# Unused filler tiles that shift where split weights and experts' operands begin in SBUF, modulo 128 bytes

## The chip, the core and the metric

The kernel runs on one NeuronCore of a Trainium2 chip. Its time is device time in microseconds (us): the median of the runs is 1857.83 us, over 3 runs from 1856.85 to 1857.92 us.

## The reference

Two transformer-like blocks follow each other on x of 256 tokens by 1024 features, all in float32. Block 1 has two layers of a token mix (a gated linear recurrence beside a latent attention) and a mixture of 16 experts, of which each token takes two of one group of four. Block 2 has a recurrent mixer, an MLP of width 4096, a local attention and a second MLP. Cut to what matters here, it is a long series of products with weights that are each used once:

```
h = rmsnorm(x, norm1_g[l]) * (1 + sc1) + sh1
x = x + g1 * token_mix(h, ..., w_in[l], ..., w_br_a[l], w_br_b[l], w_out[l])
...
he = silu(t @ w_gate[e]) * (t @ w_up[e])                 # for each expert
y  = y + combine[:, e:e+1] * (he @ w_down[e])
...
z = hn @ lru_w_in ;  x = x + g * ((scan * gelu(gate)) @ lru_w_out)
x = x + g * (square(relu(hn @ mlp_w1)) @ mlp_w2)         # twice
q, k, v, o of chunk_attention: hn @ w                     # once
```

## The kernel before, in words

**Weights.** A weight comes from HBM in pieces of 1 MiB, [128, 2048] in float32, into a tile `raw` of the pool `ring` (five buffers, and two more called `more` in the expert stages). `parts_of` (line 423) cuts a piece into parts of 1024 columns and splits each: ScalarE copies it to `whi` in float32r (line 436), VectorE subtracts that from the source and writes the rest to `wlo` (line 437). The parts take the three buffers of the pool `wsp` in turn; the recurrent stage has two more, in the pool `wse` (function `extra`), so that there three parts of five lie in `wsp`.

**Products.** Every operand is such a pair of a high and a low half, and a product is three matmuls: high by high, high by low, low by high (`mm3`, lines 447 to 449; `way_out`, lines 1654 to 1656; `first_linear`, lines 829 to 831). Each matmul has a weight load of its own ahead of it, 128 by 128, that TensorE's load queue (PEld) runs beside the matmul before it. One operand stands (it is loaded), the other moves (it is streamed):

- In `linear_gen` (names `ps_mm`), the bands (`ps_bd`), `way_out` (`acc`) and `first_linear` (`ps_f`) the weight `whi` or `wlo` stands and 256 columns of an activation move.
- In `linear_tok_gen` (`ps_mt`) the activation stands and the weight moves, 256 columns of it (512 in the two places of the latent attention, tile `cn_`).
- In the experts (`ps_e`, `py`) the gathered tokens `xg` or the turned hidden values `hT` stand and 512 columns of the weight move.

In the names of the profile the operand that moves stands first: `ps_mm<-h_hi,whi` has `whi` standing, `ps_e<-whi,xg` has `xg` standing.

**Order.** The program is written out once, in one order for each engine; the stages run one after the other, with the modulation units (`ada_unit`, line 325 on TensorE; `ada_dve`, line 299 on VectorE) put into numbered places by the table `FILL`.

**Where tiles lie.** Pools stack up in SBUF in the order in which they are opened, and within a pool each tile begins at the next multiple of 32 bytes of its partition. Nothing else sets where a tile begins. Adding up the sizes gives these beginnings modulo 128:

| tile | role | begins at, modulo 128 |
|---|---|---|
| `whi`, `wlo` of `wsp` | stand in linears, move in the experts and in `linear_tok_gen` | 64 |
| `whi`, `wlo` of `wse` (recurrent stage) | stand | 0 |
| `h_hi`, `h_lo`; `a_hi`, `a_lo` (MLP); `mg`; `hq`; `xc`; `cn_`; `y_hi` | move (`h` and `cn_` stand in `linear_tok_gen`) | 64 |
| `oa`, `ob`, `oo`, `y_lo` | move | 96 |
| `yo` | moves | 0 |
| `xg` of the first two expert groups | stands | 32 |
| `xg` of the last two, and `hT` | stand | 0 |

All slices that the products take begin whole multiples of 512 bytes further on, so that these numbers hold for them too. The small tiles `gh` (line 1123, 32 bytes, in the pool `mw`) and `q2s` (line 1754, 4 bytes) put the tiles that come after them 32 bytes off: that is how `oa`, `ob`, `oo` and `xg` come to 96 and 32.

Of the kernel before, what the change touches and what calls it, by code (L numbers as in the profile page):

```python
# [25 lines left out]
# ---------------------------------------------------------------- host layout  # L26
def cuts(kt, n):
    """The pieces a weight of kt row tiles and n columns streams in: (first row tile, row tiles, first column, columns)."""
    if kt <= 8:
        c = RING // kt // P * P  # L30
        return [(0, kt, c0, min(c, n - c0)) for c0 in range(0, n, c)]
    if kt == 11:
        return [(0, 11, c0, P) for c0 in range(0, n, P)]
    return [(k0, 8, c0, 2 * P) for c0 in range(0, n, 2 * P) for k0 in range(0, kt, 8)]


def pack(w):
    """Pieces of w, each as [128, row tiles, columns] in one row."""
    k, n = w.shape
# [5 lines left out]
# modulation units at the places in the program that have room for other than the usual number  # L45
# [11 lines left out]
def pack_mod(w, v0):  # L57
    """Four pieces for each 1024 columns of a modulation, each with two row tiles, or with two column tiles turned."""
# [45 lines left out]
def prepare(i):  # L104
# [30 lines left out]
    for l in range(DEPTH):  # L135
# [4 lines left out]
        # four heads at a time: the 32 that turn of each, then the 64 that stay  # L140
# [41 lines left out]
# ---------------------------------------------------------------- the program  # L182
def program(tc, A, out, dbg=None):
    nc = tc.nc
    from contextlib import ExitStack, nullcontext
    with ExitStack() as st:
# [3 lines left out]
        ring = pool("ring", 5)  # L190
        wsp = pool("wsp", 3)
        tmp = pool("tmp", 2)
# [5 lines left out]
        def banks(st_, stage, **tags):  # L198
            """The PSUM banks of a stage: a pool for each tag."""
# [12 lines left out]
        # ---- constants  # L212
# [45 lines left out]
        # ---- c  # L258
# [7 lines left out]
        def c_columns(i):  # L266
            """silu of a condition, 32 times"""
# [7 lines left out]
        def c_along(i):  # L275
            """silu of a condition along the free axis, on every partition"""
# [7 lines left out]
        # ---- ada: four units give the 1024 columns of a modulation, 256 in each column group of the array  # L284
# [3 lines left out]
        def ada_dve(u):  # L288
            """two column tiles of a modulation as sums along the free axis"""
# [43 lines left out]
        def ada_flush():  # L333
            """the turn of a modulation to columns, put off until the next unit's products have been queued"""
# [24 lines left out]
        def ada_site(n=1):  # L359
            """a place where units may come: the schedule says how many, n otherwise"""  # L360
# [13 lines left out]
        # ---- streaming of weights  # L374
        PRE, OWN, READY, GATE, LOADS, MORE = [], [], [], [], [], []

        def room():
            """the ring, with more buffers in turn where a stage has them"""
# [7 lines left out]
        def ready(pcs):  # L386
            """splits the next pieces that weights() will be asked for"""
# [3 lines left out]
        def prefetch(pcs):  # L391
            """loads the next pieces that weights() will be asked for"""
# [5 lines left out]
        def weights(ap, nk, nn):  # L398
            """A piece of nk row tiles and nn columns, split: w(k, c, n) -> (high, low)."""
# [16 lines left out]
        def extra(st_, n):  # L416
            """more room for split weights, in a stage that has it"""
# [42 lines left out]
        def linear_gen(pcs, kt, x, evac, fill=0, wide=False):  # L460
            """out^T tiles [128, 256]: weights stand, x (hi, lo) of [128, kt, 256] moves. With wide the first piece's
            tiles go together, for an x that is still being made."""
# [29 lines left out]
        def run(*gens):  # L492
            """Emits the generators to their ends, a step of each in turn."""
# [21 lines left out]
        def linear_tok_gen(pcs, kt, x, evac, wide=False):  # L515
            """token-major out [128 tokens, columns]: x stands, weights move."""
# [22 lines left out]
        # ---- norms  # L539
        def power(dst, src, mul=1.0):  # L540
            """(src * mul + eps) ** -1/2 of a small tile."""
# [3 lines left out]
        def rstd_tok(src, nk):  # L545
            """1/sqrt(mean + eps) of each token, [128 tokens, 2]; src(k) -> [128, 256]."""
# [11 lines left out]
        def spread(cols_):  # L558
            """columns of tokens (one for each token tile) -> [128, 256] along the free axis, in PSUM."""
# [11 lines left out]
        def stats_open(two=False, also=None, each=False):  # L571
            """The sums of squares of x, tile by tile as it gets its last sum; with two also those of x times final_g."""
# [26 lines left out]
        def stats_close(rt=None):  # L599
# [3 lines left out]
            if ST["two"]:  # L603
                ms = tmp.tile([P, 4], F32, tag="rm", name="rm")
                nc.vector.tensor_copy(ms, ST["ps"][:, 0:4])
                # r1 = (m1 + eps)^-1/2 and r1 (r1^2 m2 + eps)^-1/2 = (m2 + eps (m1 + eps))^-1/2
# [15 lines left out]
        def rstd_x(n=2):  # L622
            """the statistics at hand, along the free axis in PSUM"""
# [40 lines left out]
        def stats_late():  # L664
            """the statistics of a tile come after the products of the next"""
            if LATE_M:
                stats_add(LATE_M.pop())

        def last_linear(pcs, kt, x, gcol, fill=0, also=None):
            """a linear into x, and the statistics of x"""  # L670
# [4 lines left out]
        # ---- start: what the first norm needs  # L675
# [39 lines left out]
        def rotation():  # L715
            """cos and sin of the positions, [4 heads x 32, 256]"""
# [27 lines left out]
        # ---- lower bounds: [128, layer, lb and 1 - lb, head]  # L744
# [33 lines left out]
        # ================================================= block 1: token mix  # L778
        def first_linear(pcs, nxt, mw, mx, ma, evac):
            """The first linear, w (x a + b), while its b is on the way: w b comes in as a bias at the end."""  # L780
# [68 lines left out]
        def token_mix(l, mw):  # L849
            with ExitStack() as es:  # L850
# [7 lines left out]
                # forget gates; log f goes token-major  # L858
# [28 lines left out]
                # silu(x) = x (1 + tanh(x / 2)) / 2; that half and 128^-1/2 come in after the sums over keys  # L887
# [25 lines left out]
                # latent projections  # L913
# [10 lines left out]
                def head(hd):  # L924
# [49 lines left out]
                    # norm over the 128 values, token-major, then back  # L974
# [19 lines left out]
                # ---- MLA  # L994
# [13 lines left out]
                def latents():  # L1008
                    # the norm of c_q is a factor of each query, so it goes into the softmax scale
# [855 lines left out]
```

## Time and profile before

| what | value |
|---|---|
| median of the runs | 1857.83 us |
| span of the profiled execution | 1857.8 us |
| TensorE matmul (PE) busy | 1786.1 us, 96% |
| weight loads (PEld) busy | 1577.4 us, 85% |
| VectorE (DVE) busy | 1469.3 us, 79% |
| ScalarE (ACT) busy | 1133.2 us, 61% |
| moved from and to HBM | 485.62 MB, mean 261 GB/s |

One execution on the chip was profiled. Matmuls overlap: the next one starts before the last has ended, so that the time from one start to the next, and not the mean duration, tells how fast TensorE goes on. The view of windows gives, for a stretch of time, each engine's busy time and its instructions; the view in order of time gives every start.

### The profile page before, as it was taken

The numbers are of one execution on the slowest core, as the hardware profiler recorded it, in microseconds if no ns is written. First come the engines' busy times: TensorE is split into PE (matmuls) and PEld (weight loads), VectorE is DVE, ScalarE is ACT, GpSimd is POOL, SyncE is SP. The second block draws the span as 40 slices with busy tenths as digits, with TensorE's granted clock in tenths as the row PEclk, the third lists the DMA queues.
The fourth block names the chain that finished last, engine by engine and source line by source line (L and its number), as shares of the span: only waits on it lengthen the run. The fifth ranks groups of instructions, "written<-read, shape, count | busy, mean of one in ns | idle before, by whom it ended". The sixth has DMA issues, their size and how long they took to land. (4 is left out here: it accounts for less than half of the span.)

```text
span 1857.8 us, 31671 instructions
## 1 busy us (share of the span) xinstructions
PE 1786.1 (96%) x12430; PEld 1577.4 (85%) x12430; DVE 1469.3 (79%) x2514; ACT 1133.2 (61%) x1758; POOL 37.4 (2%) x40
## 2 busy tenths in 40 slices
PE   7999998999999899998999999899999999999999
PEld 5887897878777897897778777789899988879999
DVE  4878897998998676888998998887897667667643
ACT  4754546777777556545777777578555346546532
POOL 0000000000000000000000000000000002100000
PEclk9999998999999899999999999899999999999999
DMA  9566796797998457688797999566587763465552
GB/s 350 222 241 239 268 362 272 275 343 263 355 343 320 140 182 261 247 322 332 258 343 273 344 333 365 211 246 222 214 323 264 275 243 137 161 245 214 185 187 77
DMA packets 71727, 485.62 MB, mean 261 GB/s; under 512 B 8720, under 2 KB 10896, under 8 KB 14352
## 3 DMA queue, kind: packets, MB, share of 16 engines
q1 hardware_dynamic: 70992, 483.21, 70.0%
q8 instruction: 101, 1.65, 0.4%
q14 instruction: 58, 0.48, 0.1%
q10 hardware_dynamic: 576, 0.27, 0.1%
HBM read 482.41 MB, written 1.05 MB: 260 GB/s over the span
## 5 line engine op out<-in xcount | busy, mean ns | idle before, releaser
L437 DVE TENSOR_TENSOR wlo<-raw,whi 128x1024 fp32r<-128x1024 f32 (+1 forms) x628 | 754.3, 1210 | 172.2 <-ACT whi L436 167.8
L436 ACT CAST whi<-raw 128x1024 fp32r<-128x1024 f32 (+1 forms) x628 | 650.3, 1041 | 302.9 <-PE ps_mm L448 182.2
L447 PE MATMUL ps_mm<-h_hi,whi 128*128 128x256 f32 x1168 | 334.8, 289 | 5.5 <-ACT h_hi L643 3.5
L448 PE MATMUL ps_mm<-h_lo,whi 128*128 128x256 f32 x1168 | 333.7, 287 | 0.7 <-DVE h_lo L644 0.7
L449 PE MATMUL ps_mm<-h_hi,wlo 128*128 128x256 f32 x1168 | 332.3, 286 | 0.6 <-DVE wlo L437 0.4
L447 PEld LDWEIGHTS ps_mm<-h_hi,whi 128*128 128x128 f32 x1168 | 225.3, 194 | 11.8 <-ACT h_hi L643 5.1
L448 PEld LDWEIGHTS ps_mm<-h_lo,whi 128*128 128x128 f32 x1168 | 226.3, 194 | 2.7 <-DVE h_lo L644 0.9
L449 PEld LDWEIGHTS ps_mm<-h_hi,wlo 128*128 128x128 f32 x1168 | 225.6, 194 | 2.1 <-DVE wlo L437 1.4
L448 PE MATMUL ps_e<-wlo,xg 128*128 128x512 f32 x512 | 205.1, 401 | 2.5 <-DVE wlo L437 2.3
L447 PE MATMUL ps_e<-whi,xg 128*128 128x512 f32 x512 | 205.1, 401 | 1.1 <-ACT whi L436 1.0
L449 PE MATMUL ps_e<-whi,xg 128*128 128x512 f32 x512 | 202.6, 396 | 0.0
L447 PE MATMUL ps_mm<-a_hi,whi 128*128 128x256 f32 x512 | 145.0, 283 | 0.0
L448 PE MATMUL ps_mm<-a_lo,whi 128*128 128x256 f32 x512 | 144.9, 283 | 0.0
L449 PE MATMUL ps_mm<-a_hi,wlo 128*128 128x256 f32 x512 | 144.9, 283 | 0.0
L299 DVE SCALAR_TENSOR_TENSOR raw<-raw,cb 128x1024 f32<-128x1024 f32 x112 | 135.7, 1217 | 2.1 <-DMA raw<-in_ada_dram 2.1
L448 PEld LDWEIGHTS ps_e<-wlo,xg 128*128 128x128 f32 x512 | 96.3, 188 | 28.5 <-DVE wlo L437 7.8
L447 PEld LDWEIGHTS ps_e<-whi,xg 128*128 128x128 f32 x512 | 96.4, 188 | 23.1 <-ACT whi L436 1.8
L449 PEld LDWEIGHTS ps_e<-whi,xg 128*128 128x128 f32 x512 | 96.4, 188 | 20.8
L448 PE MATMUL py<-wlo,hT 128*128 128x512 f32 x256 | 102.3, 400 | 0.0
L449 PE MATMUL py<-whi,hT 128*128 128x512 f32 x256 | 101.1, 395 | 0.0
L447 PE MATMUL py<-whi,hT 128*128 128x512 f32 x256 | 100.7, 396 | 0.0
L448 PEld LDWEIGHTS ps_mm<-a_lo,whi 128*128 128x128 f32 x512 | 98.3, 192 | 0.0
(694 smaller groups left out, 3494.1 us busy)
## 6 DMA issues: line engine op xcount, KB each, us to landing
raw<-in_ada_dram SPq DMA_DIRECT2D x104, 1024.0 KB, 6.2
raw<-in_mw_dram SPq DMA_DIRECT2D x64, 1024.0 KB, 4.8
raw<-in_w_up_dram SPq DMA_DIRECT2D x56, 1024.0 KB, 4.8
raw<-in_w_down_dram SPq DMA_DIRECT2D x56, 1024.0 KB, 4.9
raw<-in_w_gate_dram SPq DMA_DIRECT2D x44, 1024.0 KB, 4.8
raw<-in_win_dram SPq DMA_DIRECT2D x34, 1024.0 KB, 5.0
more<-in_w_gate_dram SPq DMA_DIRECT2D x12, 1024.0 KB, 5.4
raw<-in_lwin_dram SPq DMA_DIRECT2D x11, 1024.0 KB, 6.0
```

The source lines that it names most:

```text
L299: nc.vector.scalar_tensor_tensor(w, w, 1.0, cb, op0=OP.mult, op1=OP.mult, accum_out=mod[:, m:m + 1])
L436: nc.scalar.copy(hi[:, :n], src)
L437: nc.vector.tensor_sub(lo[:, :n], src, hi[:, :n].bitcast(F32))
L447: nc.tensor.matmul(ps, ah, bh, start=start, stop=False)
L448: nc.tensor.matmul(ps, ah, bl, start=False, stop=False)
L449: nc.tensor.matmul(ps, al, bh, start=False, stop=stop)
```

## The change

It adds no instruction and takes none away. Three small filler tiles that nothing reads or writes are put between pools and tiles (`sh0` and `sh1` of 64 bytes on both sides of `wsp`, `sh2` of 32 bytes in the pool `moe`), two more of 64 bytes (`sh3`, `sh4`) on both sides of `yo`, and `gh` and `q2s` are made 128 bytes wide, of which the same columns are used as before. The comments and docstrings of the file go too.

```diff
         ring = pool("ring", 5)
+
+        def shift(p_, n, name):
+
+            p_.tile([P, n // 4], F32, tag=name, name=name, bufs=1)
+        shift(pool("sh0", 1), 64, "sh0")
         wsp = pool("wsp", 3)
+        shift(pool("sh1", 1), 64, "sh1")
         tmp = pool("tmp", 2)
...
-                gh = mw.tile([P, 8], F32, name="gh")
+                gh = mw.tile([P, 32], F32, name="gh")[:, :8]
...
                     nc.vector.tensor_copy(ovi, ov[:, :, 0])
+                    shift(mo, 32, "sh2")
...
+                    if m == 0:
+                        shift(l2, 64, "sh3")
                     yo[m] = [l2.tile([P, T], F32R, tag=f"yo{i}", name="yo", bufs=YB) for i in range(2)]
+                    if m == 0:
+                        shift(l2, 64, "sh4")
...
-                q2s = ap_.tile([P, 1], F32, name="q2s")
+                q2s = ap_.tile([P, 32], F32, name="q2s")[:, :1]
```

Adding up the sizes again gives: `wsp` at 0 (`wse` stays at 0); `h`, `a`, `mg`, `hq`, `xc`, `cn_`, `y_hi` stay at 64; `oa`, `ob`, `oo`, `y_lo` and `yo` come to 64; both pairs of `xg` and `hT` come to 0. So all products in which 256 columns move have their two operands 64 bytes apart modulo 128, and those of the experts 0 bytes apart.

## Rows read from the trace of the kernel before

**Rows 1.** The profile's page, part 1: busy time, share, instructions.

```profile
PE 1786.1 (96%) x12430; PEld 1577.4 (85%) x12430; DVE 1469.3 (79%) x2514; ACT 1133.2 (61%) x1758; POOL 37.4 (2%) x40
```

**Rows 2.** Windows: length, PE, PEld, DVE, ACT, POOL busy, clock, DMA share, GB/s.

```profile
232.00:258.00 26.00, 24.43 (x193) 22.91 (x191) 25.19 (x50) 10.41 (x16) 0.00 (x0) 1.00 0.91 354
300.00:600.00 300.00, 297.02 (x1355) 238.78 (x1354) 273.81 (x299) 228.64 (x254) 0.00 (x0) 1.00 0.83 311
...
1330.00:1420.00 90.00, 89.87 (x744) 89.30 (x743) 82.83 (x141) 53.51 (x96) 0.00 (x0) 1.00 0.80 293
1420.00:1512.00 92.00, 92.00 (x770) 92.00 (x768) 56.65 (x73) 37.02 (x42) 0.00 (x0) 1.00 0.71 252
...
1762.00:1858.00 96.00, 92.10 (x768) 91.90 (x766) 41.22 (x42) 31.64 (x32) 0.00 (x0) 1.00 0.39 132
```

**Rows 3.** Groups by line and shape: count, busy us, mean ns, idle before.

```profile
L447 PE MATMUL ps_mm<-h_hi,whi 128*128 128x256 f32 x1168 | 334.8, 289 | 5.5 <-ACT h_hi L643 3.5 <-ACT fg L867 1.5 <-ACT gate L1099 0.6
...
L447 PE MATMUL ps_e<-whi,xg 128*128 128x512 f32 x512 | 205.1, 401 | 1.1 <-ACT whi L436 1.0
...
L447 PE MATMUL ps_mm<-a_hi,whi 128*128 128x256 f32 x512 | 145.0, 283 | 0.0
...
L448 PE MATMUL py<-wlo,hT 128*128 128x512 f32 x256 | 102.3, 400 | 0.0
...
L447 PE MATMUL ps_mt<-whi,h_hi 128*128 128x256 f32 x192 | 56.9, 297 | 1.7 <-ACT h_hi L643 1.5
...
L447 PE MATMUL ps_mm<-mg_hi,whi 128*128 128x256 f32 x128 | 37.1, 291 | 0.1
...
L447 PE MATMUL ps_bd<-xc_hi,whi 128*128 128x256 f32 x62 | 18.5, 305 | 2.0 <-ACT r L1609 1.8 <-ACT ge L1572 0.2
...
L447 PE MATMUL ps_mm<-hq_hi,whi 128*128 128x256 f32 x64 | 18.3, 293 | 0.0
L447 PE MATMUL ps_mm<-oa_hi,whi 128*128 128x256 f32 x64 | 18.3, 287 | 3.1 <-DVE gate L1112 2.6 <-ACT whi L436 0.3 <-DVE gate L1116 0.2
```

**Rows 4.** In order of time, PE, the products into `acc`: start, duration.

```profile
1274.39 0.28 PE L1654 MATMUL acc<-yo,whi 128*128 128x256 f32 x1
...
1277.27 0.28 PE L1654 MATMUL acc<-yo,whi 128*128 128x256 f32 x1
...
1282.71 0.28 PE L447 MATMUL ps_bd<-xc_hi,whi 128*128 128x256 f32 x1
```

**Rows 5.** In order of time, PE, a recurrent linear whose weight lies in `wse`.

```profile
1260.46 0.28 PE L447 MATMUL ps_mm<-h_hi,whi 128*128 128x256 f32 x1
...
1261.36 0.28 PE L449 MATMUL ps_mm<-h_hi,wlo 128*128 128x256 f32 x1
```

**Rows 6.** In order of time, PE, the second attention's way out (`oo`).

```profile
1653.85 0.28 PE L447 MATMUL ps_mm<-oo_hi,whi 128*128 128x256 f32 x1
...
1656.90 0.28 PE L449 MATMUL ps_mm<-oo_hi,wlo 128*128 128x256 f32 x1
```

**Rows 7.** In order of time, PE, experts' products with `w_down`.

```profile
489.75 0.40 PE L447 MATMUL py<-whi,hT 128*128 128x512 f32 x1
...
491.62 0.40 PE L449 MATMUL py<-whi,hT 128*128 128x512 f32 x1
```

**Rows 8.** In order of time, PE, latent attention's values, second layer.

```profile
723.73 0.39 PE L449 MATMUL ps_mt<-whi,cn__6997 128*128 128x512 f32 x1
...
724.42 0.39 PE L449 MATMUL ps_mt<-whi,cn__6997 128*128 128x512 f32 x1
...
725.55 0.39 PE L448 MATMUL ps_mt<-wlo,cn__6997 128*128 128x512 f32 x1
```

**Rows 9.** VectorE's costliest groups by line and shape: count, busy us, mean ns, idle.

```profile
L437 DVE TENSOR_TENSOR wlo<-raw,whi 128x1024 fp32r<-128x1024 f32 x609 | 738.3, 1222 | 172.1 <-ACT whi L436 167.8
```

**Rows 10.** Waits within 300 to 600 us: total us, times, longest.

```profile
ACT whi L436 <- PE ps_e L449: 49.4, 111, 1.7
...
PEld ps_e L448 <- DVE wlo L437: 3.8, 9, 1.0
```

## The prediction

> **What bounds the kernel now.** I read the busy times first, then the stages in windows, then the groups by shape, then single starts in order of time. TensorE is busy 1786.1 of 1857.8 us, VectorE 1469.3, ScalarE 1133.2 [rows 1]. The windows say where that share means something [rows 2]: in the MLP stretch from 1420 to 1512 us PE is busy for all 92.00 us and VectorE for 56.65, so TensorE alone sets the pace there; in an expert stage (300 to 600) PE is busy 297.02 of 300 us but VectorE 273.81; in the branch products (232 to 258) VectorE is busy 25.19 of 26 us, more than PE, and sets the pace. No stretch is short of DMA: the highest share is 0.91.
>
> Because matmuls overlap, the mean durations of [rows 3] (289 ns and 401 ns) are not what one costs. The cost is the time from start to start. In the MLP stretch 770 matmuls touch 92 us; nearly all are 256 columns wide, and that is 0.120 us each. The whole change acts on this number, so the question is how it depends on where the two operands lie. The kernel before holds all the cases, by accident.
>
> **What the rows show of it.** In `way_out` the weight parts lie now in `wse` (0 modulo 128), now in `wsp` (64), and `yo` at 0. From 1274.39 to 1277.27 us the part lies in `wse`, 0 apart from `yo`: 24 matmuls in 2.88 us, 120.0 ns each. From 1277.27 to 1282.71 the parts lie in `wsp`, 64 apart: 48 matmuls in 5.44 us, 113.3 ns each [rows 4]. Same code, same widths, same clock. It isn't the address of one operand: in a recurrent linear with the weight in `wse` (at 0) and `h` at 64, eight steps take 0.90 us, 112.5 to 113.7 ns within the rounding [rows 5]. And 32 apart lies between: `oo` at 96 against weights at 64 takes 3.05 us for 26, 117.3 ns [rows 6].
>
> For 512 columns it runs the other way. The experts' `hT` at 0 against weights at 64 takes 1.87 us for 8, 233.8 ns [rows 7], and I find the same mean, within 1 ns, for the `xg` that is 32 apart. The only steady place at 0 apart is the latent attention's values in the second layer (`cn_` and `wsp` both at 64): 0.69 us for the first three steps, 230 ns, then 1.13 us for five, 226 ns [rows 8]. With the rounding of the last digit I take 227 ns.
>
> [...]
>
> **The change part by part.** It issues nothing and moves no instruction, so all of it is in these spacings.
>
> *Products at 0 apart that go to 64.* By [rows 3], times three for the three matmuls of a product: `h` 1168, `a` 512, `ps_mt` 192, `mg` 128, `hq` 64 and `xc` 62, together 6378; the narrow `cn_` (156), `first_linear`'s `y_hi` (128) and the `yo` on `wse` (some 105 of its 11 x 8 x 3 = 264) make it 6767, and some 230 recurrent ones on `wse` already are 64 apart. Of these 6537 I count 6100 that start within 126 ns of the one before at full clock; the others follow a wait or run at half clock, where nothing is won. 6100 x 6.67 ns = 40.7 us.
>
> *Products at 32 apart that go to 64.* `oa` and `ob` (64 x 3 each), `oo` (192) and `y_lo` (64): 640, some 570 without a wait, x 4.0 ns = 2.3 us.
>
> *Experts, from 64 and 32 to 0.* 512 x 3 in `ps_e` and 256 x 3 in `py`, 2304 [rows 3], some 2200 without a wait. From 233.8 to 227 ns: 2200 x 6.8 = 14.9 us. This is the least sure term. The nearest rows bound it: at best 226 ns [rows 8], a gain of 17 us; at worst 0 apart costs the experts what it costs 256 columns, 6.67 ns more instead of less, 240.4 ns, a loss of 14.6 us. I take the 512-wide row over the 256-wide one because it has the same shape.
>
> *VectorE, ScalarE, DMA.* Their tiles move too. The split into `wsp` at 64 and into `wse` at 0 lasts the same within 3 ns around the 1222 ns of [rows 9], so I put this at nothing. Float32 products outside this scheme (scores, transposes, some 300) may come to lie differently; at 10 ns either way that is 3 us either way, which I only put into the range.
>
> *What is late next.* The sum so far is 57.9 us, all of it TensorE's. Where VectorE is close behind, part is not paid out:
> - Branch products (232 to 258, and the same in layer 1): VectorE is at 97% [rows 2]; the gain of `oa` and `ob`, 340 x 4.0 ns = 1.4 us, goes to nothing.
> - Experts: gross 7.5 us in each stage. VectorE's 273.81 us would be 94% of 292.5. ScalarE still waits for TensorE to free a buffer of `wsp`, 49.4 us in 111 waits, and the load waits for `wlo` only 3.8 us [rows 10], so there is room, but in spurts there is none. I pay out 6.0 of 7.5, twice: 3.0 us off.
> - First half of the first MLP (1330 to 1420): gross 726 x 6.67 = 4.8 us, but VectorE's 82.83 us would be 97% of 85.2. I pay out 3.3: 1.5 us off.
> - Token mixes, recurrence and attention, gross some 17 us, VectorE at 75 to 90%: one eighth off, 2.1 us.
> - The other three MLP stretches, like the one at 1762 with VectorE at 41.22 of 96 us [rows 2], pay in full: 2300 x 6.67 = 15.3 us.
>
> 57.9 - 8.0 = 49.9 us. The profiled execution has a span of 1857.8 us, the same as the median of the runs (1857.83), so the sum is taken off that: 1808 us.
>
> **The rivals.**
> - *VectorE's splits become the bound* (chance 0.13). The three buffers of `wsp` tie the engines in a ring: TensorE frees one, ScalarE and VectorE refill it, and at 94 to 97% VectorE's other work delays the refill. For it: [rows 2] at 232 and 1330. Against it: ScalarE's 49.4 us of waiting for TensorE [rows 10]. Experts then gain nothing, the three MLP stretches keep their 15.3 us, and half of the other 25.4 us of the first term is left: 15.3 + 12.7 = 28 us, 1830 us.
> - *0 apart is bad for the experts as for the rest* (0.10). For it: it is so at 256 columns, and [rows 8] is one short place. The first two terms, less their share of the deductions, give 38 us, the experts take 14.6: 1834 us.
> - *Slower* (0.03). At 0 apart with 512 columns the next load is held until the stream lets go, over a long run and not only in a short one. The place is the 2304 expert products; it decides from 38 us / 2200 = 17 ns above now, that is 251 ns; at 264 ns (30 more) it costs 66 us: 1858 - 38 + 66 = 1886 us. Against it: none of the steps in [rows 8] is near 251.
> - *Nothing happens* (0.04): the fillers don't land where the sizes put them, or the distance isn't the cause. 1858 us. For it: fillers that nothing reads might get no room. Against it: in [rows 4] the buffer is all that changes at 1277.27.
>
> **How the numbers follow.** The forecast, 1808 us, has a chance of 0.70, with a range of its own from 1799 (all 58 us paid out) to 1820. The range: below, 1857.8 - 57.9 - 3 = 1797; above, it takes in the first rival and reaches the second's time, 1834. What lies outside is the slow and the null rival and some of the second, under 2 in 10. What a measurement of this kernel can tell from no change is about 0.2%, or 3.7 us: faster by more is the forecast and the first two rivals, 0.70 + 0.13 + 0.10 = 0.93; the same is 0.04; slower is 0.03.
>
> **What would show it.** In the order of time after the change: starts 113.3 ns apart in the MLP (`a_hi`), the last stretch of 768 such matmuls some 5 us shorter, `oo` also at 113.3, and `acc` at 113.3 throughout instead of by turns; expert products 227 ns apart, an expert stage of 294 us. VectorE's busy time stays at 1469 us and its share grows; the load's waits for `wlo` in an expert stage grow from 3.8 us to some 5 to 8. Wrong it would be if `a_hi` stays at 120.0 ns (the null rival), if the experts stand at 240 (the second) or above 251 (the slow one), or if spacings fall as said and the waits for `wlo` take up the gain (the first).

## The result, and the profile after

The changed kernel takes 1831.17 us (median of four runs, 1827.80 to 1833.09) beside 1857.34 us before (four runs, 1856.59 to 1857.92): a ratio of 0.9855, 95% interval 0.9844 to 0.9867. The time lies inside the forecast's range and the sign is right, but of the 49.9 us of the sum only some 26 came. The profiled execution has a span of 1828.0 us (before 1857.8).

Part 1 of the page of the kernel after, beside [rows 1]:

```profile
PE 1748.5 (96%) x12430; PEld 1548.3 (85%) x12430; DVE 1465.6 (80%) x2514; ACT 1130.7 (62%) x1758; POOL 37.4 (2%) x40
```

The instructions are the same in number, and VectorE's and ScalarE's work is as it was; TensorE's busy time fell by 37.6 us, so the gain is TensorE's, as forecast. The stages of the kernel after in windows, in the columns of [rows 2] (branch products, first expert stage, first MLP's first linear, its second, second MLP's second):

```profile
228.00:253.00 25.00, 23.57 (x190) 22.11 (x189) 23.63 (x44) 9.74 (x13) 0.00 (x0) 1.00 0.93 360
297.60:595.00 297.40, 293.97 (x1367) 240.57 (x1365) 273.08 (x299) 229.16 (x255) 0.00 (x0) 0.99 0.83 316
1330.00:1401.70 71.70, 71.30 (x608) 70.60 (x607) 66.65 (x113) 42.56 (x76) 0.00 (x0) 1.00 0.86 322
1401.70:1493.00 91.30, 91.12 (x774) 90.92 (x774) 57.44 (x75) 37.34 (x43) 0.00 (x0) 1.00 0.71 254
1737.00:1828.00 91.00, 87.28 (x770) 87.09 (x769) 41.68 (x42) 31.97 (x32) 0.00 (x0) 1.00 0.40 140
```

The last two rows hold the finding. They are the same 768 matmuls, `a` against `w2`, once in each MLP, at the same full clock and both with TensorE busy nearly throughout. From the first start to the last they take 90.8 us in the first MLP (before 92.0) and 87.0 in the second (before 92.1). One got a quarter of its 5.1 us, the other all of it. Single starts in order of time show why (kernel after, PE: start, duration, line, product):

```profile
480.70 0.39 PE L454 MATMUL py<-wlo,hT 128*128 128x512 f32 x1
...
482.06 0.39 PE L454 MATMUL py<-wlo,hT 128*128 128x512 f32 x1
...
1295.13 0.28 PE L1666 MATMUL acc<-yo,whi 128*128 128x256 f32 x1
...
1299.89 0.28 PE L1666 MATMUL acc<-yo,whi 128*128 128x256 f32 x1
...
1401.18 0.28 PE L453 MATMUL ps_mm<-h_hi,whi 128*128 128x256 f32 x1
...
1401.75 0.28 PE L455 MATMUL ps_mm<-h_hi,wlo 128*128 128x256 f32 x1
1401.86 0.28 PE L453 MATMUL ps_mm<-a_hi,whi 128*128 128x256 f32 x1
...
1403.16 0.28 PE L455 MATMUL ps_mm<-a_hi,wlo 128*128 128x256 f32 x1
...
1450.03 0.28 PE L454 MATMUL ps_mm<-a_lo,whi 128*128 128x256 f32 x1
...
1451.09 0.28 PE L454 MATMUL ps_mm<-a_lo,whi 128*128 128x256 f32 x1
...
1627.78 0.28 PE L453 MATMUL ps_mm<-oo_hi,whi 128*128 128x256 f32 x1
...
1629.19 0.28 PE L453 MATMUL ps_mm<-oo_hi,whi 128*128 128x256 f32 x1
...
1760.09 0.28 PE L455 MATMUL ps_mm<-a_hi,wlo 128*128 128x256 f32 x1
...
1761.11 0.28 PE L455 MATMUL ps_mm<-a_hi,wlo 128*128 128x256 f32 x1
```

- The experts' `py`: six steps in 1.36 us, 227 ns, where [rows 7] had 233.8.
- `acc` from 1295: 42 steps in 4.76 us, 113.3 ns; `a` in the second MLP (1760): nine in 1.02 us, 113.3.
- `a` in the first MLP (1450): nine in 1.06 us, 117.8 ns; `oo` (1628): twelve in 1.41 us, 117.5.
- At 1401.8 the step goes from 114 ns (five in 0.57 us) to 118 (eleven in 1.30 us) without any pause, at the change from `h` to `a`, and stays there for the whole linear.

So 64 apart modulo 128 this kernel has two steps, 113.3 and 117.8 ns, and each lasts. I then counted all the steps from start to start that neither wait (up to 126 ns for 256 columns, 242 for 512) nor run at the lower granted clock (0.5, where 256 columns take 213 ns, before at 0 apart and after at 64 alike):

| steps, operands apart modulo 128 | before: count, mean ns | after: count, mean ns | us, after less before |
|---|---|---|---|
| 256 columns, 0 | 6170, 119.7 | 90, 118.5 | |
| 256 columns, 64 | 399, 115.4 | 7089, 115.5 | |
| 256 columns, 32 | 584, 117.5 | 0 | |
| 256 columns, all three | 853.4 us | 829.5 us | -23.9 |
| 512 columns | 2154, 233.4 | 2149, 228.2 | -12.4 |
| steps with a wait, both widths | | | +9.8 |
| steps at the lower clock | 150 | 111 | -7.8 |
| other products | | | +4.4 |

The sum is -29.9 us; the spans differ by 29.8. (A second execution of the kernel after, `again` below, has 150 steps at the lower clock, as many as before, so I don't put their 7.8 us down to the change.)

The waits of the first expert stage of the kernel after, as [rows 10] (who waits, for whom: total us, times, longest):

```profile
ACT whi L442 <- PE ps_e L455: 45.9, 110, 1.7
...
PEld ps_e L454 <- DVE wlo L443: 4.1, 9, 1.0
```

VectorE is hardly later there than before (3.8 us, nine times), and its split lasts what it did in [rows 9]:

```profile
L443 DVE TENSOR_TENSOR wlo<-raw,whi 128x1024 fp32r<-128x1024 f32 x609 | 737.1, 1221 | 152.0 <-ACT whi L442 135.6 <-PE ps_mm L454 1.1
```

### The profile page after: what moved, and what is told of

It reads as the page before. It is cut to its first block, busy times and chain, and to the rows that moved or that the text cites. A ratio compares the mean times of both kernels' runs of the same rounds, so it can differ in the third digit from the quotient of the medians.

```text
span 1828.0 us, 31671 instructions
## 1 busy us (share of the span) xinstructions
PE 1748.5 (96%) x12430; PEld 1548.3 (85%) x12430; DVE 1465.6 (80%) x2514; ACT 1130.7 (62%) x1758; POOL 37.4 (2%) x40
## 5 line engine op out<-in xcount | busy, mean ns | idle before, releaser
L453 PE MATMUL ps_mm<-h_hi,whi 128*128 128x256 f32 x1168 | 329.7, 285 | 5.5 <-ACT h_hi L649 3.5
L454 PE MATMUL ps_mm<-h_lo,whi 128*128 128x256 f32 x1168 | 327.9, 282 | 0.7 <-DVE h_lo L650 0.7
L455 PE MATMUL ps_mm<-h_hi,wlo 128*128 128x256 f32 x1168 | 327.4, 282 | 1.0 <-DVE wlo L443 1.0
L454 PEld LDWEIGHTS ps_mm<-h_lo,whi 128*128 128x128 f32 x1168 | 222.6, 191 | 2.6 <-DVE h_lo L650 0.9
L455 PEld LDWEIGHTS ps_mm<-h_hi,wlo 128*128 128x128 f32 x1168 | 221.6, 190 | 3.6 <-DVE wlo L443 2.7
L453 PE MATMUL ps_e<-whi,xg 128*128 128x512 f32 x512 | 202.7, 396 | 1.2 <-ACT whi L442 1.0
L455 PE MATMUL ps_e<-whi,xg 128*128 128x512 f32 x512 | 200.3, 391 | 0.0
L455 PEld LDWEIGHTS ps_mm<-a_hi,wlo 128*128 128x128 f32 x512 | 96.0, 187 | 0.4 <-DVE wlo L443 0.4
```

The source lines that it names most:

```text
L453: nc.tensor.matmul(ps, ah, bh, start=start, stop=False)
L454: nc.tensor.matmul(ps, ah, bl, start=False, stop=False)
L455: nc.tensor.matmul(ps, al, bh, start=False, stop=stop)
```

## The experiments

My theory of the missing 24 us: 64 apart has a second lasting step of 117.8 ns, and about half of the products took it ((115.5 - 113.3) / 4.5). Rivals: VectorE's cover was thinner than forecast, so that the gain turned into waits; or the distance counts modulo 256, so that of the products "64 apart modulo 128" those at 64 are quick and those at 192 slow (in the kernel after, `h` is at 64, `a` and `oo` at 192). Distances below are modulo 256 unless said otherwise: the start of the standing operand less that of the moving one.

**linears_only**: the experts' distances put back, the rest of the change kept.

```diff
                 csl = mo.tile([P, NG, 4], F32, name="csl")
+                shift(mo, 96, "sh5")
...
-                    shift(mo, 32, "sh2")
+                    pass
```

> The changed kernel, but the experts' operands put back to the distances of before (one more filler of 96 bytes ahead of `xg`, `sh2` left out): 32 and 64 apart again, 256-wide products as in the changed kernel. Theory 'two steps' (at 64 apart a 256-wide product has two lasting step lengths, 113.3 and some 117.7 ns, and the second took the missing gain; the experts' 227 ns are real and paid out): expert products back at 233.5 ns, 2200 x 5.3 ns = 12 us lost, 1843 us. Theory 'cover gone' (VectorE's splits set the pace, the experts gained nothing): 1831 us as the changed kernel.

Measured: 1842.26 us (1840.22 to 1844.68), ratio 0.9923 (0.9906 to 0.9940). The experts' steps are back at 233.3 ns (twelve in 2.80 us; this kernel, PE, in order of time):

```profile
479.62 0.39 PE L454 MATMUL ps_e<-wlo,xg 128*128 128x512 f32 x1
...
482.42 0.39 PE L454 MATMUL py<-wlo,hT 128*128 128x512 f32 x1
```

Without the experts' part 11.1 us of the gain are gone, near the 12.4 of the count. Were the cover gone in the expert stages, nothing would have been lost.

**experts_only**: the kernel before with two fillers in the experts' pool alone.

```diff
                 csl = mo.tile([P, NG, 4], F32, name="csl")
+                shift(mo, 32, "sh5")
...
                     nc.vector.tensor_copy(ovi, ov[:, :, 0])
+                    shift(mo, 32, "sh2")
```

> The kernel before with two fillers of 32 bytes in the pool `moe` alone: the experts' standing operands 0 apart from the weights, all 256-wide products as before. 'Two steps': expert products at 227 to 228 ns, an expert stage 5 us shorter, 12 us in all, 1845 us; 256-wide products at 120.0. 'Cover gone': 1857 us, as before, with the waits of the load for `wlo` up.

Measured: 1858.02 us (1856.36 to 1858.91), ratio 1.0001 (0.9991 to 1.0010). The time is the one that "cover gone" gave, but not its sign: the load's waits for `wlo` in the first expert stage are 3.8 us in nine, as before. "Two steps" missed the time. With `wsp` still at 64, 0 apart modulo 128 is here 128 modulo 256, and 2147 steps have a mean of 232.5 ns: eleven in 2.57 us in this kernel:

```profile
479.80 0.40 PE L450 MATMUL ps_e<-whi,xg 128*128 128x512 f32 x1
...
482.37 0.40 PE L452 MATMUL ps_e<-whi,xg 128*128 128x512 f32 x1
```

So the short step for 512 columns (227 ns in the kernel after) isn't at 0 modulo 128, as the change (and my prediction) put it: of 0 and 128 modulo 256 only 0 had it.

**flip**: the kernel after with `sh0` and `sh1` at 192 bytes, so that every distance to a weight in `wsp` moves by 128: `h` to 192, `a` and `oo` to 64, the experts to 128.

```diff
-        shift(pool("sh0", 1), 64, "sh0")
+        shift(pool("sh0", 1), 192, "sh0")
-        shift(pool("sh1", 1), 64, "sh1")
+        shift(pool("sh1", 1), 192, "sh1")
```

> The changed kernel with `wsp` another 128 bytes on (fillers of 192 instead of 64 on both sides): all distances the same modulo 128, but modulo 256 what was 64 is now 192 and what was 192 is 64. If modulo 128 is all that counts, spacings and time stay as they are within the scatter: 1831 us, about half of the 256-wide steps at 117.7. If the distance modulo 256 picks the step (64 the short one, 192 the long one): `h` goes from mostly 113.3 to mostly 117.7 (3300 x 0.5 x 4.4 ns = 7 us lost), `a`, `mg`, `hq`, `oo` the other way (4 us won), 1834 us, with the first MLP's second linear at 113.3. 'Cover gone': 1831 us, whatever the steps do. Experts at 128 modulo 256: 227 ns if 128 is the period, else something else.

Measured: 1837.80 us (1837.47 to 1840.26), ratio 0.9894 (0.9878 to 0.9911). The experts at 128 take 232.5 ns again, which is 2123 x (232.5 - 228.1) = 9.3 us, more than the 6.6 us that it is slower than the kernel after. At 256 columns the distance biases the step but does not fix it. Of the runs of six steps of `h` at 192 that wait for nothing, 17% are at 113.3 ns; in the kernel after, at 64, it was 65%. But `a` at 64 did what it did at 192: slow in the first MLP (90.33 us for its 768), quick in the second (87.03).

**plus64**: the kernel after with one filler of 128 bytes (`sh6`) and `gh` and `sh3` widened by 128, so that every product with a standing weight is at 64 modulo 256.

```diff
+         shift(pool("sh6", 1), 128, "sh6")
...
-                gh = mw.tile([P, 32], F32, name="gh")[:, :8]
+                gh = mw.tile([P, 64], F32, name="gh")[:, :8]
...
-                        shift(l2, 64, "sh3")
+                        shift(l2, 192, "sh3")
```

> The changed kernel with a filler of 128 bytes after the pool `rou`, `gh` 256 bytes wide and `sh3` of 192 bytes: every 256-wide product whose weight stands is 64 apart modulo 256 (only `ps_mt`, where the activation stands, is at 192). If the distance modulo 256 picks the step: nearly all of the 256-wide steps at 113.3, up to 13 us won over the changed kernel, 1820 to 1827 us. If modulo 128 is all that counts and the step is picked by chance at the start of a stretch: 1831 us, half of the steps at 117.7. 'Cover gone': 1831 us, with shorter steps and longer waits for `wlo`.

Measured: 1831.12 us (1829.32 to 1835.15), ratio 0.9856 (0.9839 to 0.9872), the kernel after to the microsecond. `oo` went to 113.3, but `a` is at 117.8 in both MLPs, and of the runs of six of `h`, at 64 as in the kernel after, only 38% are short. The rival of 64 against 192 falls: the distance alone does not choose between the two.

**again**: the kernel after once more, unaltered.

> The changed kernel, unaltered, profiled a second time. Theory 'a toss at each start' (both step lengths last, and a stretch takes one of them as TensorE starts it anew after a wait): the same stretches differ from the first profile, above all the second linears of the two MLPs, which had 117.7 and 113.3 ns there; a stretch of 768 is 3.4 us longer or shorter by that, the whole within 1826 to 1834 us. Theory 'the addresses decide': the same stretches take the same steps as in the first profile.

Measured: 1827.67 us. Long stretches mostly take the step that they took before (`a` slow in the first MLP, 90.34 us, and quick in the second, 87.01); some shorter ones took the other (of the runs of six of `acc`, 64% were short, now 36%). It isn't fixed by the program alone, nor is it a toss each time.

The two linears of `a`, 768 matmuls each, over all the profiled executions, from the first start to the last:

| kernel | `a` apart | first MLP, us | second MLP, us |
|---|---|---|---|
| before | 0 | 92.04 | 92.10 |
| after | 192 | 90.78 | 87.01 |
| again | 192 | 90.34 | 87.01 |
| linears_only | 192 | 90.56 | 90.42 |
| flip | 64 | 90.33 | 87.03 |
| plus64 | 64 | 90.33 | 90.42 |
| lead32 | 64 | 90.33 | 90.34 |
| lead_slow | 192 | 90.33 | 90.33 |
| set2 | 64 | 89.07 | 90.34 |
| set3 | 64 | 90.33 | 86.94 |

At 64 and at 192 alike there are mostly two values, 87.0 (113.3 ns) and 90.4 (117.8), 3.4 us apart. `set2`'s 89.07 is a stretch that changed step on its way, and the first 90.78 has one wait of 0.3 us in it.

**map1**: products alone, without the kernel's other work, at 16 distances, eight starts each.

> Not the kernel's work: only products, in the order high-high, high-low, low-high, on tiles that stay. The standing operand begins 0, 16, 32 to 240 bytes after the moving one modulo 256; 8 starts for each distance with 72 matmuls of 256 columns, then 4 with 24 of 512; at every other start TensorE waits for ScalarE, at the others only one product of 128 columns comes between. 'A toss at each start': at 64 and 192 some starts lead to 113.3 and some to 117.7 ns that last to the end of the 72, at 0 and 128 always 120.0; at 64 more of the short ones than at 192. 'The addresses decide': one step for each distance. Of the distances that no kernel here had (16, 48, 80 and so on) both leave open whether one of them has the short step alone. 512 columns: 227 ns at 0, 232 to 234 at 32, 64, 96 and 128.

Measured, 256 columns, ns: 120.0 at 0, 144 and 160 (bar one start), 119.9 to 120.2 at 112; 113.3 to 113.4 at 64, and nowhere else; between 116.5 and 118.8 at the others (117.8 at 192). 512 columns: 226.7 at 0, 144 and 240; 228.6 to 232 at 80, 176, 192 and 208; 233.1 to 234.7 at the rest, 64 and 128 among them. Each distance keeps its step over its starts, with few exceptions. Two stretches of 12 steps of this kernel, at 64 and at 192, 1.36 and 1.42 us:

```profile
48.98 0.28 PE L56 MATMUL b<-xh,wl 128*128 128x256 f32 x1
...
50.34 0.28 PE L56 MATMUL b<-xh,wl 128*128 128x256 f32 x1
...
119.74 0.28 PE L56 MATMUL b<-xh,wl 128*128 128x256 f32 x1
...
121.16 0.28 PE L56 MATMUL b<-xh,wl 128*128 128x256 f32 x1
```

The products alone say what the change wanted: 64 short for 256 columns (113.3 ns), 0 short for 512 (226.7). But each distance came behind the one 16 bytes below it, so this map can't tell a distance from the way into it.

**map2**: products alone again, at 64 and at 192, each begun in several ways, three times.

> Not the kernel's work: products of 256 columns in the same order as in the map of distances, at distance 64 (steps of 113.3 ns in the map) and 192 (117.8 in the map), 96 in a row, three times, after different ways in: without a pause after 48 products at distance 0, 32, 64, 96, 128 or 192; after an operand that ScalarE and VectorE make tile by tile while the products wait; after four small float32 products; after a modulation unit's four float32 products; after a wait for the `lo` half of the weight. Theory 'the way in decides, and the step lasts': 64 after 192 without a pause stays at 117.8, 192 after 64 stays at 113.3, and the entry with an operand in the making, which is how the MLP's first linear starts, gives 117.8 at 64 in some cases. Theory 'the distance decides': 113.3 at 64 and 117.8 at 192 after every way in, from the first few products on, and the long steps at 64 in the kernel come from something that runs beside TensorE there.

Measured: both distances have both steps, 113.3 and 117.8 ns, and here the way in chooses. Straight after products at 0 apart, 64 takes 117.8 and 192 takes 113.3; straight after 32, 96 or 128 it is the other way round; three times out of three each, and the step lasts to the end of the 96 products. After 192 in its long step, 64 stays at 117.8. After four small float32 products 64 takes 117.8, and after a wait for `wlo` 113.3 once and 117.8 twice. So both 113.3 and 117.8 came at "64 modulo 128", and in these runs the products ahead of a stretch set which one it got.

**lead32** and **lead_slow**: that theory turned into a kernel. Six products whose results are overwritten stand ahead of the MLPs' stretches, in `lead32` (on plus64) at 32 apart, in `lead_slow` (on the kernel after) at 0 apart for `h` and 32 for `a`, to make the stretches short in the one and long in the other.

```diff
+                    if lead and lead[0] == i and c == 0:
+                        by = lead[1].rearrange("p k t -> p (k t)")[:, lead[2] // 4:lead[2] // 4 + T]
+                        for _ in range(6):
+                            nc.tensor.matmul(ps, w(0, c, P)[0], by, start=True, stop=True)
```

> The kernel of run plus64 (all 256-column products with a weight standing at 64 apart modulo 256), with six products more whose results are overwritten, 32 bytes apart (the moving slice begins 32 bytes later), ahead of four stretches: the second piece of each MLP's first linear and the first piece of each MLP's second. Theory 'the way in decides and the step lasts': what follows six products at 32 without a pause takes 113.3 ns, as in the products measured alone, so the 891 + 761 + 761 products that took 117.7 in plus64 take 113.3: 2413 x 4.4 = 10.6 us less, 24 x 0.12 = 2.8 us more, about 1823 us beside plus64's 1831. Rival 'the place in the program decides (what ScalarE and VectorE do meanwhile)': the stretches stay at 117.7 and the time is 1831 + 2.8 = 1834. Rival 'six are too few': steps as in plus64 at least in part, between 1826 and 1834.

> The kernel after, with six products more at the same four places, their results overwritten: 0 apart ahead of the first linears (which are at 64), 32 apart ahead of the second linears (which are at 192 modulo 256). Theory 'the way in decides and the step lasts': alone, 64 after 0 and 192 after 32 both went to 117.8, so the MLP of block 1, whose 708 + 761 products took 113.3 in after, goes to 117.7: 1469 x 4.4 = 6.5 us more, and 24 x 0.12 = 2.8 us for the added products, about 1840 us beside 1831. Rival 'the place decides': the steps stay as in after, and the time is 1831 + 2.8 = 1834.

Measured: lead32 1836.79 us (1834.69 to 1840.88), ratio 0.9889 (0.9872 to 0.9905); lead_slow 1836.01 us (1833.28 to 1839.84), ratio 0.9882 (0.9866 to 0.9899). Both missed. In lead32 both stretches of `a` (90.33 and 90.34 us) and that of `h` in the second MLP stayed long (`h` in the first MLP changes its step several times, with the lead and without; in the kernel after 54 of its runs of six are short and 61 long), and ahead of the first `a` the six products turned a short step into a long one (PE, in order of time; the row with x6 is the lead):

```profile
1400.98 0.28 PE L456 MATMUL ps_mm<-h_hi,wlo 128*128 128x256 f32 x1
...
1401.66 0.28 PE L456 MATMUL ps_mm<-h_hi,wlo 128*128 128x256 f32 x1
1401.78 0.87 PE L495 MATMUL ps_mm<-h_hi,whi 128*128 128x256 f32 x6
1402.48 0.28 PE L454 MATMUL ps_mm<-a_hi,whi 128*128 128x256 f32 x1
...
1403.19 0.28 PE L454 MATMUL ps_mm<-a_hi,whi 128*128 128x256 f32 x1
```

Ahead of it six steps take 0.68 us (113.3 ns), behind it six take 0.71 (117.5). In lead_slow `a` of the second MLP went from short to long (87.01 to 90.33 us), as meant, but `h` stayed short (113.3 ns). The scheduler had drawn those two leads in among the products of the piece before, so those places test little. Still, the last two or three products at 0 stand straight ahead of `h` there, and behind them it takes 113.3, where the products alone took 117.8 (second MLP; x2 is the end of the lead):

```profile
1653.48 0.40 PE L494 MATMUL ps_mm<-h_hi,whi 128*128 128x256 f32 x2
...
1654.19 0.28 PE L453 MATMUL ps_mm<-h_hi,whi 128*128 128x256 f32 x1
...
1655.21 0.28 PE L453 MATMUL ps_mm<-h_hi,whi 128*128 128x256 f32 x1
```

From 1654.19 nine steps take 1.02 us. "Products at 32 bring 113.3" is refuted as a rule. The same with 24 products (lead24) has no time.

**map3**: products alone; a lead of n products between two runs at 64.

> Products alone (none of the kernel's work). Each case: 48 products at 32 apart or at 0 apart, 48 at 64, then a lead of n products (32 apart or 0 apart, all with one weight slice, or taking turns as the kernel's groups do), then 48 at 64 again; 32 cases, twice, begun after a short and after a long pause. From the products measured before: 64 after 48 at 32 takes 113.3 ns, 64 after 48 at 0 takes 117.8. Theory A 'the distance just before sets the step': after every lead at 32 the step is 113.3 and after every lead at 0 it is 117.8, whatever n. Theory B 'the count sets it': the step after a lead changes with n at one distance, the same both times; then six leading products in the kernel were merely an unlucky number. Theory C 'any lead that is no multiple of a group upsets it': 113.3 stays only where the lead takes turns or counts three or six. Rival D 'a step once begun outlasts a lead': the step after the lead is that of before it, 113.3 in the cases begun at 32 and 117.8 in those begun at 0.

Measured: in these runs the count decides (theory B). A lead at 0 apart, of one to six products, left 117.8 behind it in 24 cases out of 24 (in 14 of them, and in all four with one product, the step ahead was 117.8 already). A lead at 32 of 1, 3, 4 or 24 kept the step there was, short or long, one case of n = 1 excepted; a lead of 2, 5 or 6 turned it into the other, from short to long and from long to short, every time; whether its products took turns as a group does made no difference. Two products at 32 after a short run and after a long one (PE of this kernel; x2 is the lead):

```profile
52.13 0.28 PE L58 MATMUL b<-xh,wl 128*128 128x256 f32 x1
...
52.81 0.28 PE L58 MATMUL b<-xh,wl 128*128 128x256 f32 x1
52.93 0.40 PE L68 MATMUL b<-xh,wh 128*128 128x256 f32 x2
53.17 0.28 PE L56 MATMUL b<-xh,wh 128*128 128x256 f32 x1
...
54.11 0.28 PE L58 MATMUL b<-xh,wl 128*128 128x256 f32 x1
...
332.92 0.28 PE L56 MATMUL b<-xh,wh 128*128 128x256 f32 x1
...
333.63 0.40 PE L68 MATMUL b<-xh,wh 128*128 128x256 f32 x2
...
333.99 0.28 PE L57 MATMUL b<-xl,wh 128*128 128x256 f32 x1
...
334.90 0.28 PE L56 MATMUL b<-xh,wh 128*128 128x256 f32 x1
```

From 52.13 six steps take 0.68 us, after the lead eight take 0.94 (117.5); from 332.92 six take 0.71, after the lead eight take 0.91 (113.8). The lead of lead32 shown above, where six turned short into long, fits that. Its fourth place does not: ahead of the second MLP's `a` six at 32 came behind a long stretch and a modulation unit's small products, and `a` stayed long (90.34 us).

**set2** and **set3**: that rule in the kernel. The lead on plus64 is one product at 0 (to set the long step), three at 64, and two at 32 (to turn it) in set2, three at 32 (to keep it) in set3.

```diff
+                        for o in [64] + [0] * 3 + [32] * 2:
+                            nc.tensor.matmul(ps, w(0, c, P)[0], flat[:, o // 4:o // 4 + T], start=True, stop=True)
```

> The kernel of run plus64 with a lead of six products, whose results are overwritten, at four places: ahead of the third piece of each MLP's first linear and of the first piece of each MLP's second. One is 0 apart, three are 64 apart, two are 32 apart, and the stretch behind is 64 apart. Theory 'the count sets the phase', as the products alone showed it: any lead at 0 left 117.8 behind it, and two products at 32 turned 117.8 into 113.3. So the second linears' 763 and 761 products and some 600 of block 1's first linear take 113.3 where plus64 had 117.7: 2100 x 4.4 = 9.3 us less, 24 x 0.12 = 2.8 more, about 1825 us beside plus64's 1831. Rival 'in the kernel something else sets it' (the writes of ScalarE and VectorE, the stretch of three 64s too short): steps as in plus64, about 1834.

> As set2 with three products at 32 apart in place of two. In the products alone three at 32 kept the step there was. Theory 'the count sets the phase': the lead's product at 0 sets 117.8 and three at 32 leave it, so all the stretches behind the leads take 117.7, about 1831 + 28 x 0.12 = 1834 us. Rival 'leads at 32 of any count help' or 'something else sets it': set3 and set2 have the same steps and the same time within 1 us.

Measured: set2 1831.01 us (1826.82 to 1835.41), ratio 0.9840 (0.9819 to 0.9862); set3 1833.80 us (1831.02 to 1836.19), ratio 0.9858 (0.9837 to 0.9878). Of the four places of set2 one is short behind its lead, where all should be; of set3's three are long, as they should be, and one is short. In set2, ahead of `h` in the first MLP and in the second:

```profile
1317.11 0.88 PE L495 MATMUL ps_mm<-h_hi,whi 128*128 128x256 f32 x6
...
1318.29 0.28 PE L455 MATMUL ps_mm<-h_lo,whi 128*128 128x256 f32 x1
...
1319.42 0.28 PE L456 MATMUL ps_mm<-h_hi,wlo 128*128 128x256 f32 x1
...
1658.28 0.87 PE L495 MATMUL ps_mm<-h_hi,whi 128*128 128x256 f32 x6
...
1658.98 0.28 PE L454 MATMUL ps_mm<-h_hi,whi 128*128 128x256 f32 x1
...
1660.16 0.28 PE L455 MATMUL ps_mm<-h_lo,whi 128*128 128x256 f32 x1
```

Ten steps in 1.13 us (113) behind the first lead, ten in 1.18 (118) behind the second, with the same six products in between. The first had a short stretch ahead of it, the second a long one. So here one product at 0 did not wipe out what was there before, as I took it to do from the products alone, where a single one had never stood behind a short stretch. The theory, as put on record, fell.

Read afterwards by what stood ahead, though, the eight places agree. The lead of set2 kept the step in four of four (once short, three times long); that of set3 turned it in four of four, three times from short to long, and once from long to short. That once, ahead of `a` in the second MLP of set3 (x4 a modulation unit, x7 the lead):

```profile
1742.17 0.51 PE L348 MATMUL ps_mod<-c_sel,ada_s 128*128 128x4 f32 x4
1742.53 1.08 PE L495 MATMUL ps_mm<-h_hi,whi 128*128 128x256 f32 x7
...
1743.92 0.28 PE L455 MATMUL ps_mm<-a_lo,whi 128*128 128x256 f32 x1
...
1744.94 0.28 PE L455 MATMUL ps_mm<-a_lo,whi 128*128 128x256 f32 x1
```

Nine steps in 1.02 us, 113.3 ns, where plus64 had 117.8 at this place. That would say that the count of a lead shifts the step in the kernel too, from the step that is there; but it is a reading of eight places after the fact, not a test. A version that uses set3's lead only where a long step stands ahead would follow from this; it was not tried.

No version tried is faster than the kernel after by more than the runs can tell: plus64 and set2 have its time.

## Why the prediction was right in sign and range, and wrong by half in size

**What held.** That in this kernel the spacing of matmuls depends on where their operands lie, and that TensorE's time pays for it: 37.6 us less busy time with the same instructions. linears_only, too, differs from the kernel after by fillers alone, and takes 11 us more (1842.26 beside 1831.17 us). The range, 1797 to 1834 us, held because it was drawn to take in two rivals; the forecast's own, 1799 to 1820, missed. Of the signs, the last 768 steps came 5.1 us shorter and the experts' step at 227 ns; `oo` (117.5 ns) and a third of `acc` (117.8) did not come to 113.3.

**The experts** (14.9 us forecast, 12.4 by the count, 11.1 by linears_only). The step came out at 227 ns in steady runs, from 233.2 rather than 233.8 on two thirds of the products, and the mean after is 228.1 with the steps around a change of weight part. The choice of [rows 8] over the 256-wide rows was right; the second rival (0 apart bad for the experts too) fell, and the slow one's held load was not shown: it put the experts' steps at 251 ns and more, and their mean is 228. But the reason was only half understood: 0 modulo 128 is not enough (experts_only and flip, 232.5 ns at 128). `cn_` and `wsp` in [rows 8] lay 0 apart modulo 256, and I had no row at 128.

**The step that failed** is the first term of the sum, "6100 x 6.67 ns = 40.7 us", with the second, "x 4.0 ns". The count was right (7089 steps at 64 afterwards); the size was not. 113.3 ns was read off 48 steps of `acc` in [rows 4] and eight in [rows 5], and taken as the step at 64 apart. It is one of two. The forecast of 43.0 us for both terms became 23.9: the 7089 steps have a mean of 115.5, and 7089 x (115.5 - 113.3) = 15.6 us of the 19.1 us missing; the other 3.5 us are of the size of two small things, that steps 0 apart were 119.7 and not 120.0 ns on the mean (6170 x 0.3 = 1.9 us), and that this count has 26 more steps after (7179 for 7153, 3.0 us). The trace of before had said so: its 399 steps at 64 apart have a mean of 115.4 ns, within a tenth of what came. The long step stood in it over whole stretches, at the very product and distance of [rows 4] (kernel before, PE, in order of time; `acc` with the weight in `wsp`):

```profile
1297.60 0.28 PE L1655 MATMUL acc<-yo,whi 128*128 128x256 f32 x1
...
1300.19 0.28 PE L1656 MATMUL acc<-yo,wlo 128*128 128x256 f32 x1
```

That is 22 steps in 2.59 us, 117.7 ns. I built the term on the 113.3 of 1277 alone. With the group's mean the term is 6100 x (119.7 - 115.4) = 26 us.

**What is late next** (8.0 us held back). The steps with waits grew by 9.8 us, most of it in the 256-wide ones. That is near the forecast though it lies otherwise: an expert stage is 5.0 and 5.2 us shorter (6.0 each were to be paid out), and the load's waits for `wlo` there went from 3.8 to 4.1 us where 5 to 8 were expected. The first rival, VectorE's splits as the bound, gave 1830 us, which is the time that came, but for a reason that did not happen: in the first MLP's second linear VectorE is busy for 57 of 91 us and one product in 768 waits for it, 0.3 us, yet they got 1.3 us of their 5.1. A time that agrees with a rival does not make it true; its place does, and here the loss is in steps that wait for nothing. The other products, put at 3 us either way with no row for the 10 ns each, took 4.4 us more, and 1.3 more in `again`.

**What stays open.** What chooses between 113.3 and 117.8 in the kernel. The runs show that it isn't the distance modulo 256 alone (plus64, flip), though that weighs: `oo` at 192 was long in all four executions that have it there (117.5 ns in the kernel after), at 64 short in four of five (113.3 in plus64). They show that a stretch mostly keeps its step until products at another distance or a pause come between (of the 18 stretches of `a` at 64 and 192 only that of set2 with 89.07 us lies between the two values), and that in the products alone the count of such products turns it (map3). In the kernel the eight places of set2 and set3 fit a count, but read afterwards, and lead32's fourth place and lead_slow's `h` do not fit map3's. Which step the first stretch begins with, and why some stretches change between two executions (again), the runs don't tell. Why 64 apart has two steps and why 0 apart modulo 128 has two for 512 columns was not measured, and no trace shows inside TensorE's reads.

## What to carry to other kernels

In this kernel, with TensorE busy for 96% of the span, the start-to-start step was 2 to 6% shorter at one distance between the standing and the moving operand than at another, at no cost in instructions: for these float32r products 64 apart modulo 128 paid at 256 columns (113.3 or 117.8 ns against 120.0 at 0), and 0 modulo 256 at 512 (227 ns against 233 at 64 and 232.5 at 128). Whether another kernel has such a difference is read from the steps of its own trace. Size such a term by the mean of every step that the trace before has at the new distance, not by its cleanest stretch; where a group has two values, as here, count on both. Try distances beyond 128 bytes too, since 0 and 128 modulo 256 differed here at 512 columns, and don't count on the shorter of two steps: three tries to force it gained nothing over the plain change (plus64 and set2 have its time, lead32 is 5.6 us slower).

## What the runs showed of the hardware that was not expected

- Two lasting steps at one and the same distance, in the kernel after: 113.3 and 117.8 ns at 256 columns, 64 apart modulo 128. Over the executions with `a` at 64 or 192 modulo 256 its 768 matmuls took 86.9 to 87.0 or 90.3 to 90.8 us, and once something in between (89.1, set2).
- In map3, products alone, a lead of 2, 5 or 6 products at 32 apart turned the one into the other, a lead of 1, 3, 4 or 24 kept it (one exception at 1), and any lead at 0 apart left 117.8 (24 of 24). In the kernel the last does not hold: behind products at 0 `h` took 113.3 (lead_slow).
- 512 columns: 226.7 ns at 0, 144 and 240 apart modulo 256 and 233.1 to 234.7 at 32, 64 and 128 (map1); in the kernels 228.1 at 0 (after) and 232.5 at 128 (flip, experts_only). 256 columns: 120.0 at 0 (before, map1), 113.3 or 117.8 at 64 and 192 (after, map2).
- VectorE's split of a weight part took 1222 ns before, with `whi` and `wlo` of `wsp` at 64 modulo 128, and 1221 after, with them at 0.
